# A hybrid recurrent encoder: score matmuls under a high priority, with the backward scores of both halves as one group

## The chip, the cores and the metric

The kernel runs on one core of a Trainium2 chip. The metric is device time in microseconds (us) of one execution. A core has five engines that run their own instruction streams and wait for each other by semaphores: TensorE (PE in the profile, its weight loads PEld), VectorE (DVE), ScalarE (ACT), GpSimd (POOL) and SyncE (SP), which here starts most of the transfers.

## What is computed

Two layers on 1024 tokens of width 1024, in float32. Each projects its input, mixes along the sequence, projects back and adds with a layer norm. The mixers of layer 0 are a dilated window attention (8 heads) and a gated linear attention (GLA, 4 heads with 256 values); the mixer of layer 1 is an HGRN2 recurrence (12 heads with 128 values). GLA and HGRN share this recurrence, run forward and backward:

```python
def _chunk_gated_scan(q, k, v, log_g):
    ...
    b = jnp.cumsum(log_g, axis=2)
    ref = b[:, :, CHUNK // 2 - 1:CHUNK // 2]
    s = jnp.einsum('bnthk,bnshk->bnhts', q * jnp.exp(b - ref), k * jnp.exp(ref - b))
    s = jnp.where(np.tril(np.ones((CHUNK, CHUNK), bool)), s, 0.0)
    o_intra = jnp.einsum('bnhts,bnshv->bnthv', s, v)
    b_last = b[:, :, -1]
    q_dec = q * jnp.exp(b)
    k_dec = k * jnp.exp(b_last[:, :, None] - b)

    def step(state, xs):
        qd, kd, vc, bl = xs
        o = jnp.einsum('bthk,bhkv->bthv', qd, state)
        state = jnp.exp(bl)[..., None] * state + jnp.einsum('bthk,bthv->bhkv', kd, vc)
        return state, o
    ...

def bidirectional_gated_scan(q, k_fwd, g_fwd, k_bwd, g_bwd, v):
    fwd = _chunk_gated_scan(q, k_fwd, v, g_fwd)
    ...
    return fwd + bwd - diag
```

## The kernel before

All weights and activations of the projections are split into a high and a low part, and each product takes three matmuls: L237 to L239 for projections with features on the partitions ("pj"), L249 to L251 for those with tokens there, L271 to L273 for the out-projections ("po"), whose results VectorE adds to the residual (L276). They are most of TensorE's work. ScalarE rounds a raw weight tile (the cast, L199), VectorE makes the low part (L200); ScalarE or VectorE evacuates a finished projection (L712 and others).

The recurrence works on tiles of 128 tokens, in two halves of four tiles (hf 0 and 1) and two directions (d = 1 backward, d = 0 forward). The function `core` of a `ScanHead` gives a list of units in the order (1,1), (1,0), (0,0), (0,1), written (d,hf) from here on. For each come three units, and for d = 0 a fourth:

- `prep`: on VectorE a running sum of the log gate (L743), differences (L746, L750), and scaled queries and keys: qi (L756), ki (L1056 in GLA, L1129 in HGRN), k3 (L787), q1 and k1 (L792, L793), q2 and k2 (L797, L798), q3 (L799). ScalarE makes the exponentials (through L158), GpSimd small factors (L763 to L783). GLA's log gate begins with a matmul (L1044) that takes a bank of the scores' PSUM tag.
- `keys`: three or four transposes of k3 on TensorE (L809, PSUM tag tr, one buffer), a copy of them on ScalarE (L812, k3T), state matmuls (L818, tag kv, one buffer), and the state updates on VectorE (L828 for the first, L830 for the others).
- `scores`: 32 small matmuls (L844) of 32 output partitions each, into one PSUM buffer of the tag s (two buffers). They need ki, qi, k1, q1, k2 and q2, of which k2 is made last. Then S is taken from PSUM: by ScalarE for d = 1 (L870), by VectorE under a mask for d = 0 (L873).
- `output` (d = 0): o from S and v (L888), from the forward states (L890) and the backward ones (L892), tag o; a norm with two matmuls of ones (L905, L906, tag tr) and the multiplication by the gate (L912 to L917).

GLA heads have nbuf = 1 (one buffer for most of these tiles), HGRN heads nbuf = 2. Heads are named H0 to H11 in layer 1 and by their number in GLA; H2, H4, H6, H8 and H10 have an out-projection of the pair of heads before them beside their core, and token projections.

The units of a head's core are merged with the projections of the next heads and the out-projections of earlier ones by a table of fractions (`WIN`, `LAST`, `merge`), which gives the program's order. A scheduler then orders each engine's instructions, once, when the kernel is built: by their place in the program, and earlier than that by up to 3000 places for what stands under `high_priority(offset=3000)`; the evacuations, the weight casts and other short steps are under it before the change, too. On the chip every engine takes its instructions in that order. `issue_after` ties an instruction to come after a named one of the same engine.

Of the kernel before, what the change touches and what calls it, by code (L numbers as in the profile page):

```python
# [2 lines left out]

# [12 lines left out]
P = 128  # L16
# [677 lines left out]
class ScanHead(Item):  # L694
# [135 lines left out]
                    nc.vector.scalar_tensor_tensor(dst, old, r["dec"][:, t, :], kv[:, j, :],  # L830
                                                   op0=ALU.mult, op1=ALU.add)

    def scores(self, d, hf):

        T, nc = self.T, self.T.nc
        mm = nc.tensor.matmul
        r = self.pr[d, hf]
        ev, od = d, 1 - d
        first, last = d, 1 - d
        X = T.ps.tile([P, 4, P], F32, tag="s", name="s", bufs=2)  # L840

        def block(t, s0, t0, n, k, q):

            mm(X[s0:s0 + 32, t, t0:t0 + n], k, q, start=True, stop=True)  # L844

        def far(t, i):

            k2, q2 = (r[x][:, t].rearrange("p a c -> p (a c)") for x in ("k2", "q2"))
            block(t, 64 * first + 32 * i, 64 * last, 64, k2[:, 32 * i:32 * i + 32], q2)

        def near(t, i):

            n = 2 * t + i
            block(t, 64 * i + 32 * ev, 64 * i + 32 * od, 32, r["k1"][:, n, :], r["q1"][:, n, :])

        def own(t, i, e):

            s0 = 64 * i + 32 * e
            t0, n = (s0, 32) if e == ev else (64 * i, 64)
            block(t, s0, t0, n, r["ki"][:, t * P + s0:t * P + s0 + 32], r["qi"][:, t * P + t0:t * P + t0 + n])  # L860

        for t in range(4):
            far(t, ev), far(t, od), own(t, last, ev), own(t, last, od)
            near(t, first), own(t, first, od), near(t, last), own(t, first, ev)
        dst = self.S[:, hf * 4:hf * 4 + 4, :]
        for i in range(2):
            ss = slice(64 * i, 64 * i + 64)
            cs = slice(0, P) if i == first else slice(64 * last, 64 * last + 64)
            if d == 1:
                nc.scalar.copy(dst[ss, :, cs], X[ss, :, cs])  # L870
            else:
                mask = T.mask[ss, cs].unsqueeze(1)
                nc.vector.copy_predicated(out=dst[ss, :, cs], data=X[ss, :, cs],  # L873
                                          mask=mask.broadcast_to([64, 4, cs.stop - cs.start]))

    def output(self, hf):

# [42 lines left out]
    def core(self):  # L920
        pool = self.pool

        def begin():
            if self.mate:
                self.v = self.mate.v
            self.pr = {}
            self.S = pool.tile([P, NT, P], F32, tag="S", name="S", bufs=1)
            self.stb = pool.tile([P, NT - 1, self.V], F32, tag="stb", name="stb", bufs=1)
            self.stf = {}
            self.y, self.held = {}, {}  # L930

        units = [begin, lambda: self.activate(1)]
        for d, hf in ((1, 1), (1, 0), (0, 0), (0, 1)):
            if (d, hf) == (0, 0):
                units.append(lambda: self.activate(0))
            units.append(lambda d=d, hf=hf: self.prep(d, hf))
            units.append(lambda d=d, hf=hf: self.keys(d, hf))
            units.append(lambda d=d, hf=hf: self.scores(d, hf))
            if (d, hf) == (0, 0):
                units.append(lambda: self.activate(2))  # L940
            if d == 0:
                units.append(lambda hf=hf: self.output(hf))
            if (d, hf) == (0, 0):
                n = len(units)
        return units, n / len(units)
# [186 lines left out]
def trunk_kernel(tc, x, x_t, w_in_ab, gla_gate_up, gla_gate_bias, gla_norm, w_out_ab, w_in_c, hgrn_lower_bounds,  # L1132
                 hgrn_norm, w_out_c, rel_bias, ln_gain, ln_bias, onehot, ident, mask, out):
    nc = tc.nc
    with ExitStack() as ctx:
# [127 lines left out]
        def step(items, i, after=None, spill=()):  # L1263
# [6 lines left out]
            late, n = it.late(), it.urgent  # L1270
            m = n + 2 if "LATE2" in w else len(late)
            core, p = it.core()
            st = [(core, 0.0, 1.0), (late[:n], *w["URGENT"]), (late[n:m], *w["LATE"])]
            if late[m:]:
                st.append((late[m:], *w["LATE2"]))
# [93 lines left out]
```

## Time and profile before

| | |
|---|---|
| runs (us) | 1990.79, 1993.53, 1996.21; median 1993.53 |
| profiled execution (us) | 1989.75, its span 1988.0 |
| mean granted clock of TensorE | 0.995 of full |
| busy: TensorE, its weight loads | 1909.4 us (96%), 1568.1 us (79%) |
| busy: VectorE, ScalarE, GpSimd | 1317.6 us (66%), 1015.1 us (51%), 345.8 us (17%) |
| score matmuls (L844) | 64 groups of 32; each matmul shows as two records, 4096 in all |

A time line has a row for each instruction, or for some alike in a row (x3): its start in us from the start of the span, its duration, engine, line, what it writes from what it reads, and in brackets the idle time of its engine just before it with the instruction that ended it. A matmul's duration is modelled and overlaps the next one's, so on TensorE one reads the distance from start to start. The groups by line give busy time, the mean of one and the idle time before them. The chain that ended last is followed back from the last instruction; its shares tell which engine sets the time.

### The profile page before, as it was taken

How to read it: one execution, taken by the hardware profiler on the slowest of the kernel's cores; microseconds unless marked ns; L12 is line 12 of the kernel's file. 1: busy time of each engine (PE TensorE's matmuls, PEld its weight loads, DVE VectorE, ACT ScalarE, POOL GpSimd, SP SyncE). 2: the span in 40 equal slices, each digit the busy share in tenths (PEclk: the TensorE clock that was granted, in tenths of full speed). 3: DMA queues.
4: the chain of work that ended last, by engine and by line, in shares of the span. 5: the costliest groups of instructions: out<-in, count | busy, mean ns of one | idle time of the engine just before them, and what ended most of it. 6: DMA issues, size and time to landing. Idle time of an engine off the chain costs nothing.

```text
span 1988.0 us, 35443 instructions
## 1 busy us (share of the span) xinstructions
PE 1909.4 (96%) x13887; PEld 1568.1 (79%) x13887; DVE 1317.6 (66%) x2757; ACT 1015.1 (51%) x1851; POOL 345.8 (17%) x856
## 2 busy tenths in 40 slices
PE   7999999999999999989899999999999999999997
PEld 4777777787787878867778888888888888888875
DVE  4687878775776575677667646655764664666477
ACT  5665666653554343444556445535544642654473
POOL 0210202001211011121423111111311210131133
PEclk9999999999999999999999999999999999999999
DMA  8321212123121212112311211121121112012112
GB/s 230 76 50 38 45 38 44 33 75 100 38 54 49 70 49 70 48 43 75 123 39 43 69 54 38 39 80 33 33 85 44 33 49 75 27 39 90 38 44 85
DMA packets 142868, 118.60 MB, mean 60 GB/s; under 512 B 15302, under 2 KB 122566, under 8 KB 142700
## 3 DMA queue, kind: packets, MB, share of 16 engines
q1 hardware_dynamic: 128875, 98.36, 16.9%
q0 software_dynamic: 4512, 11.47, 2.3%
q10 hardware_dynamic: 9312, 6.50, 1.1%
q8 instruction: 109, 1.79, 0.4%
q14 instruction: 60, 0.48, 0.1%
HBM read 108.19 MB, written 8.11 MB: 59 GB/s over the span
## 4 chain that ended last, share of the span: by engine, by line
PE 46%; DVE 8%; ACT 4%; DMA 2%; issue 2%; POOL 1%; DVEq 0%; ACTq 0%; POOLq 0%
PE pj L237 9%; PE pj L238 8%; PE pj L239 8%; PE kv L818 3%; DVE g L743 2%; PE po L271 2%; PE po L272 2%; PE po L273 2%; PE s L844 2%; PE pj L249 1%; PE pj L250 1%; PE pj L251 1%; PE o L888 1%; PE o L892 1%; PE o L890 1%
## 5 line engine op out<-in xcount | busy, mean ns | idle before, releaser
L237 PE MATMUL pj<-xH,wH 128*128 128x512 f32 x1280 | 510.7, 399 | 5.0 <-DVE kl L531 2.3
L238 PE MATMUL pj<-xL,wH 128*128 128x512 f32 x1280 | 506.3, 396 | 0.0
L239 PE MATMUL pj<-xH,wL 128*128 128x512 f32 x1280 | 505.7, 395 | 0.0
L199 ACT CAST wH<-wraw 128x512 fp32r<-128x512 f32 x248 | 153.6, 619 | 298.8 <-PE pj L238 180.0
L200 DVE TENSOR_TENSOR wL<-wraw,wH 128x512 fp32r<-128x512 f32 x248 | 172.4, 695 | 200.6 <-ACT wH L199 187.9
L237 PEld LDWEIGHTS pj<-xH,wH 128*128 128x128 f32 x1280 | 240.6, 188 | 53.2 <-issue 3.0
L239 PEld LDWEIGHTS pj<-xH,wL 128*128 128x128 f32 x1280 | 240.7, 188 | 45.5
L238 PEld LDWEIGHTS pj<-xL,wH 128*128 128x128 f32 x1280 | 240.9, 188 | 44.3 <-DVE xL L348 0.4
L763 POOL TENSOR_TENSOR eT<-gE 128x16 f32<-128x16 f32 x64 | 29.6, 463 | 1037.0 <-ACT gE L158 1037.0
L249 PE MATMUL pj<-wH,xH 128*128 128x256 f32 x640 | 182.1, 285 | 2.3 <-ACT E L712 1.9
L250 PE MATMUL pj<-wL,xH 128*128 128x256 f32 x640 | 180.8, 283 | 0.0
L251 PE MATMUL pj<-wH,xL 128*128 128x256 f32 x640 | 180.6, 283 | 0.0
L276 DVE TENSOR_TENSOR z<-z,po 128x512 f32<-128x512 f32 x200 | 134.9, 682 | 65.1 <-PE po L273 64.2
L271 PE MATMUL po<-woH,yH 128*128 128x512 f32 x336 | 138.4, 421 | 9.4 <-ACT woH L217 5.8
L272 PE MATMUL po<-woL,yH 128*128 128x512 f32 x336 | 134.7, 401 | 0.5 <-DVE woL L218 0.5
L273 PE MATMUL po<-woH,yL 128*128 128x512 f32 x336 | 132.1, 394 | 0.0
L249 PEld LDWEIGHTS pj<-wH,xH 128*128 128x128 f32 x640 | 122.1, 191 | 6.2 <-ACT E L712 2.3
L250 PEld LDWEIGHTS pj<-wL,xH 128*128 128x128 f32 x640 | 122.1, 191 | 2.9
L251 PEld LDWEIGHTS pj<-wH,xL 128*128 128x128 f32 x640 | 122.0, 191 | 2.6
L271 PEld LDWEIGHTS po<-woH,yH 128*128 128x128 f32 x336 | 61.8, 188 | 33.4 <-ACT woH L217 10.7
L818 PE MATMUL kv<-v,k3T 128*128 128x128 f32 (+1 forms) x448 | 80.0, 313 | 8.1 <-DVE stb L830 5.2
L217 ACT CAST woH<-wraw 128x512 fp32r<-128x512 f32 x80 | 47.5, 617 | 78.2 <-PE po L273 26.7
(230 smaller groups left out, 3852.7 us busy)
## 6 DMA issues: line engine op xcount, KB each, us to landing
wraw<-in_w_in_c_dram SPq DMA_DIRECT2D x152, 256.0 KB, 2.9
wraw<-in_w_in_ab_dram SPq DMA_DIRECT2D x96, 256.0 KB, 2.9
wraw<-in_w_out_c_dram SPq DMA_DIRECT2D x44, 256.0 KB, 2.7
wraw<-in_w_out_ab_dram SPq DMA_DIRECT2D x40, 256.0 KB, 2.6
z<-in_x_dram ACTq DMA_DIRECT2D x8, 512.0 KB, 5.6
strip<-line POOLq DMA_DIRECT2D x8, 448.0 KB, 5.7
park<-sp SPq DMA_DIRECT2D x14, 256.0 KB, 2.0
out_dram<-z SPq DMA_DIRECT2D x6, 512.0 KB, 2.6
```

The source lines that it names most:

```text
L199: self.nc.scalar.copy(h, raw)
L200: self.nc.vector.tensor_tensor(lo, raw, h.bitcast(F32), op=ALU.subtract)
L237: mm(ps[:m], wH, xH[:, k, :], start=(k == 0), stop=False)
L238: mm(ps[:m], wH, xL[:, k, :], start=False, stop=False)
L239: self.lastmm = mm(ps[:m], wL, xH[:, k, :], start=False, stop=(k == last)).ins
L249: self.nc.tensor.matmul(o, xH, wH, start=(k == 0 and i % 2 == 0), stop=False)
L250: self.nc.tensor.matmul(o, xH, wL, start=False, stop=False)
L251: self.lastmm = self.nc.tensor.matmul(o, xL, wH, start=False, stop=(k == KT - 1 and i % 2 == 1)).ins
L271: mm(ps, yH[:, ts], h, start=(b == 0), stop=False)
L272: mm(ps, yH[:, ts], lo, start=False, stop=False)
L273: mm(ps, yL[:, ts], h, start=False, stop=(b == nb - 1))
L818: nc.tensor.matmul(kv[:, j, :], k3T[:, t, :], self.val(hf * 4 + t), start=True, stop=True)
```

## The change

The matmuls of `scores` come under the high priority, tied in order by `issue_after`, so that no other matmul comes between those of a group; the copies from PSUM to S are made after it, at the program's own place. For nbuf = 2 (HGRN) and d = 1, one unit after `prep` and `keys` of (1,0) issues the scores of (1,0) and then those of (1,1).

```diff
--- before.py
+++ after.py
@@ -1,5 +1,5 @@
 import math
-from contextlib import ExitStack
+from contextlib import ExitStack, nullcontext
 
 import concourse.bass as bass
 import concourse.tile as tile
@@ -830,10 +830,19 @@
                     nc.vector.scalar_tensor_tensor(dst, old, r["dec"][:, t, :], kv[:, j, :],
                                                    op0=ALU.mult, op1=ALU.add)
 
-    def scores(self, d, hf):
+    def scores(self, d, hfs):
+
+        tc, done = self.T.tc, []
+        with tc.high_priority(offset=3000):
+            for hf in hfs:
+                with tc.issue_after(self.lastmm) if done else nullcontext():
+                    done.append(self.score_tiles(d, hf))
+        for fn in done:
+            fn()
+
+    def score_tiles(self, d, hf):
 
         T, nc = self.T, self.T.nc
-        mm = nc.tensor.matmul
         r = self.pr[d, hf]
         ev, od = d, 1 - d
         first, last = d, 1 - d
@@ -841,7 +850,7 @@
 
         def block(t, s0, t0, n, k, q):
 
-            mm(X[s0:s0 + 32, t, t0:t0 + n], k, q, start=True, stop=True)
+            self.lastmm = nc.tensor.matmul(X[s0:s0 + 32, t, t0:t0 + n], k, q, start=True, stop=True).ins
 
         def far(t, i):
 
@@ -862,16 +871,20 @@
         for t in range(4):
             far(t, ev), far(t, od), own(t, last, ev), own(t, last, od)
             near(t, first), own(t, first, od), near(t, last), own(t, first, ev)
-        dst = self.S[:, hf * 4:hf * 4 + 4, :]
-        for i in range(2):
-            ss = slice(64 * i, 64 * i + 64)
-            cs = slice(0, P) if i == first else slice(64 * last, 64 * last + 64)
-            if d == 1:
-                nc.scalar.copy(dst[ss, :, cs], X[ss, :, cs])
-            else:
-                mask = T.mask[ss, cs].unsqueeze(1)
-                nc.vector.copy_predicated(out=dst[ss, :, cs], data=X[ss, :, cs],
-                                          mask=mask.broadcast_to([64, 4, cs.stop - cs.start]))
+
+        def take():
+            dst = self.S[:, hf * 4:hf * 4 + 4, :]
+            for i in range(2):
+                ss = slice(64 * i, 64 * i + 64)
+                cs = slice(0, P) if i == first else slice(64 * last, 64 * last + 64)
+                if d == 1:
+                    nc.scalar.copy(dst[ss, :, cs], X[ss, :, cs])
+                else:
+                    mask = T.mask[ss, cs].unsqueeze(1)
+                    nc.vector.copy_predicated(out=dst[ss, :, cs], data=X[ss, :, cs],
+                                              mask=mask.broadcast_to([64, 4, cs.stop - cs.start]))
+
+        return take
 
     def output(self, hf):
 
@@ -935,7 +948,9 @@
                 units.append(lambda: self.activate(0))
             units.append(lambda d=d, hf=hf: self.prep(d, hf))
             units.append(lambda d=d, hf=hf: self.keys(d, hf))
-            units.append(lambda d=d, hf=hf: self.scores(d, hf))
+            both = self.nbuf == 2 and d == 1
+            if not both or hf == 0:
+                units.append(lambda d=d, hfs=(0, 1) if both else (hf,): self.scores(d, hfs))
             if (d, hf) == (0, 0):
                 units.append(lambda: self.activate(2))
             if d == 0:
```

The scheduler turns this into the following moves. TensorE in head H3, just ahead of the backward scores (pj are projections for later heads, tr the transposes of k3). Before, the group of (1,1) follows its transposes:

```order
L238 MATMUL pj<-xL,wH 128x512
L239 MATMUL pj<-xH,wL 128x512
L809 MATMUL tr<-ident,k_12895 128x128 x4
L844 MATMUL s<-q_12901,k_12902 32x64 x2
L844 MATMUL s<-qi,ki 32x32
L844 MATMUL s<-qi,ki 32x64
L844 MATMUL s<-q_12897,k_12898 32x32
```

With the change the joined group comes first (its first matmul reads k2 of (1,0)):

```order
L237 MATMUL pj<-xH,wH 128x512
L238 MATMUL pj<-xL,wH 128x512
L853 MATMUL s<-q_12988,k_12989 32x64 x2
L853 MATMUL s<-qi,ki 32x32
L853 MATMUL s<-qi,ki 32x64
L853 MATMUL s<-q_12984,k_12985 32x32
```

and the transposes of (1,1) come behind it, among projections:

```order
L238 MATMUL pj<-xL,wH 128x512
L239 MATMUL pj<-xH,wL 128x512
L809 MATMUL tr<-ident,k_12895 128x128 x4
L237 MATMUL pj<-xH,wH 128x512
L238 MATMUL pj<-xL,wH 128x512
```

The joined group moved ahead of the transposes; counted in projections from the (0,1) group of the head before, it stands at the 111th and the transposes at the 127th, where they and the first scores stood at the 120th. The norm's matmuls of the head before (L905, L906 of its second half) end at the 22nd instead of the 16th.

VectorE in H3, from the first state update of (1,1) on (stb are the backward states, g the log gates that the next preparation sums). Before:

```order
L828 COPY stb<-kv 128x128
L830 SCALAR_TENSOR_TENSOR stb<-stb,dec,kv 128x128
L743 SCALAR_TENSOR_TENSOR g<-restart,g 128x512
L830 SCALAR_TENSOR_TENSOR stb<-stb,dec,kv 128x128
L746 COPY gt<-g 128x32
L743 SCALAR_TENSOR_TENSOR g<-restart,g 128x512
L830 SCALAR_TENSOR_TENSOR stb<-stb,dec,kv 128x128
L750 TENSOR_TENSOR g<-g,gt 128x16x16
L746 COPY gt<-g 128x32
L750 TENSOR_TENSOR g<-g,gt 128x16x16
```

With the change:

```order
L828 COPY stb<-kv 128x128
L743 SCALAR_TENSOR_TENSOR g<-restart,g 128x512
L830 SCALAR_TENSOR_TENSOR stb<-stb,dec,kv 128x128
L746 COPY gt<-g 128x32
L743 SCALAR_TENSOR_TENSOR g<-restart,g 128x512
L830 SCALAR_TENSOR_TENSOR stb<-stb,dec,kv 128x128
L750 TENSOR_TENSOR g<-g,gt 128x16x16
L830 SCALAR_TENSOR_TENSOR stb<-stb,dec,kv 128x128
L746 COPY gt<-g 128x32
L750 TENSOR_TENSOR g<-g,gt 128x16x16
```

The first scan (L743) now stands ahead of the second update, and an L750 ahead of the fourth.

TensorE in H3, in the middle of the (0,1) group. Before, three state matmuls cut it:

```order
L844 MATMUL s<-qi,ki 32x64
L844 MATMUL s<-q_13315,k_13316 32x32
L844 MATMUL s<-qi,ki 32x32
L818 MATMUL kv<-v,k3T 128x128 x3
L844 MATMUL s<-q_13319,k_13320 32x64 x2
L844 MATMUL s<-qi,ki 32x32
L844 MATMUL s<-qi,ki 32x64
L844 MATMUL s<-q_13315,k_13316 32x32
```

With the change its end and what follows are:

```order
L853 MATMUL s<-q_13315,k_13316 32x32
L853 MATMUL s<-qi,ki 32x64
L853 MATMUL s<-q_13315,k_13316 32x32
L853 MATMUL s<-qi,ki 32x32
L905 MATMUL o<-q_12981,stb 128x128
L901 MATMUL o<-S,v 128x128
L903 MATMUL o<-q_13156,stf 128x128
L905 MATMUL o<-q_12981,stb 128x128
```

Over the whole program the 64 groups stand in 78 pieces before and in 52 with the change, none of them cut by another matmul. Here the group is in one piece, stands between output matmuls of (0,0), and the three state matmuls come later.

## Rows read from the trace of the kernel before

**Rows 1.** The page, busy time by engine, and the chain that ended last by engine:

```profile
PE 1909.4 (96%) x13887; PEld 1568.1 (79%) x13887; DVE 1317.6 (66%) x2757; ACT 1015.1 (51%) x1851; POOL 345.8 (17%) x856
...
PE 46%; DVE 8%; ACT 4%; DMA 2%; issue 2%; POOL 1%; DVEq 0%; ACTq 0%; POOLq 0%
```

**Rows 2.** Groups by line, shapes apart: busy us, mean ns | idle before, and its releasers:

```profile
L844 PEld LDWEIGHTS s<-q,k 128*32 128x32 f32 x2048 | 62.1, 110 | 19.7 <-issue 16.1 <-DVE k L798 0.8 <-PE pj L238 0.7
...
L818 PE MATMUL kv<-v,k3T 128*128 128x128 f32 x336 | 49.4, 287 | 8.1 <-DVE stb L830 5.2 <-ACT k3T L812 0.8 <-ACT S L870 0.4
...
L809 PE MATMUL tr<-ident,k 128*128 128x128 f32 x224 | 35.5, 275 | 11.5 <-DVE k L787 11.5
```

**Rows 3.** Time line of TensorE, scores of (1,0), H2: start us, us, work:

```profile
1193.30 0.40 PE L239 MATMUL pj<-xH,wL 128*128 128x512 f32 x1
1193.62 0.25 PE L844 MATMUL s<-q,k 128*32 128x64 f32 x2
...
1194.54 0.23 PE L844 MATMUL s<-qi,ki 128*32 128x32 f32 x2
1194.69 0.50 PE L237 MATMUL pj<-xH,wH 128*128 128x512 f32 x1
1195.03 0.39 PE L238 MATMUL pj<-xL,wH 128*128 128x512 f32 x1
1195.26 0.40 PE L239 MATMUL pj<-xH,wL 128*128 128x512 f32 x1
```

**Rows 4.** The same, the split (0,1) group of H2:

```profile
1204.35 0.24 PE L844 MATMUL s<-qi,ki 128*32 128x64 f32 x3
1204.73 0.94 PE L818 MATMUL kv<-v,k3T 128*128 128x128 f32 x6
```

**Rows 5.** Time line of all engines, preparation and (1,1) of H3:

```profile
1214.96 0.62 ACT L199 CAST wH<-wraw 128x512 fp32r<-128x512 f32 x1 [0.26 <-PE pj L238]
...
1215.49 0.59 ACT L712 ACTIVATE E<-pj 128x512 f32<-128x512 f32 x1
...
1234.72 0.39 PE L237 MATMUL pj<-xH,wH 128*128 128x512 f32 x1
...
1234.78 0.42 DVE L798 TENSOR_TENSOR k<-ki,Gk 128x256 f32<-128x256 f32 x1
...
1236.77 0.60 PE L809 MATMUL tr<-ident,k 128*128 128x128 f32 x4
```

**Rows 6.** The same, H4, a head with an out-projection:

```profile
1313.20 0.28 PE L249 MATMUL pj<-wH,xH 128*128 128x256 f32 x1
...
1313.55 0.42 DVE L798 TENSOR_TENSOR k<-ki,Gk 128x256 f32<-128x256 f32 x1
```

**Rows 7.** The same, H0:

```profile
1001.64 0.42 DVE L798 TENSOR_TENSOR k<-ki,Gk 128x256 f32<-128x256 f32 x1
...
1003.16 0.60 PE L809 MATMUL tr<-ident,k 128*128 128x128 f32 x4
```

**Rows 8.** The same, state matmuls and updates of (1,1) and (1,0), H3:

```profile
1243.36 1.16 PE L818 MATMUL kv<-v,k3T 128*128 128x128 f32 x8
...
1245.14 1.22 DVE L743 TENSOR_TENSOR_SCAN g<-restart,g 128x512 f32<-128x512 uint8 x1
...
1247.75 0.32 DVE L830 SCALAR_TENSOR_TENSOR stb<-stb,dec,kv 128x128 f32<-128x128 f32 x1
...
1247.99 0.42 DVE L750 TENSOR_TENSOR g<-g,gt 128x256 f32<-128x256 f32 x1
...
1248.22 0.91 PE L818 MATMUL kv<-v,k3T 128*128 128x128 f32 x6 [0.49 <-DVE stb L830]
```

**Rows 9.** TensorE's waits in GLA, and a window (us, busy by engine, granted clock):

```profile
706.39 0.52 PE L809 MATMUL tr<-ident,k 128*128 128x128 f32 x3 [1.02 <-DVE k L787]
...
902.73 0.80 PE L888 MATMUL o<-S,v 128*128 128x128 f32 x2 [2.65 <-DVE S L873]
...
904.00:912.00 8.00, 7.24 (x48) 6.96 (x47) 7.40 (x7) 4.13 (x8) 6.75 (x4) 0.74 0.12 36
```

## The prediction

> **What bounds the kernel now.** I read the page first, then the groups by line, then time lines of single heads. TensorE is busy 96% of the span, and it holds 46% of the chain that ended last, VectorE 8% [rows 1]: the kernel is a stream of TensorE instructions in one fixed order, and time changes only where that stream waits or changes from one kind of matmul to another. So I look for such places. The weight loads of the score matmuls waited for k2 (L798) 0.8 us in the whole run; the 16.1 us beside it are "issue", a price of changing kind and no wait for data [rows 2]. The transposes waited 11.5 us for k3 (L787), the state matmuls 8.1 us, mostly for the state updates on VectorE (L830) that free their one PSUM buffer [rows 2].
>
> **The change, part by part.** The order shows that it adds and removes no instruction on any engine. Score groups move on TensorE, and copies and parts of preparation move on VectorE and ScalarE behind them. I cost places, not instructions.
>
> *Changes of kind.* Projection to projection takes 0.23 us from start to start; projection to score 0.32, the last score to a projection 0.15 where one score after another takes 0.03 (all 32 start between 1193.62 and 1194.54), and the step behind that 0.34 [rows 3]. One excursion so costs 0.10 on the way in and twice 0.11 on the way out, 0.32 in all. Joining the two backward groups of an HGRN head saves one excursion. But the order shows what comes back: the transposes of (1,1), which led straight into its scores, now stand between projections (+0.12), one state matmul of (0,0) is left alone behind its scores (+0.18), and (0,1) goes into the outputs at other points (+0.07). I take 0 for the head; the ends are -0.3 and +0.2, or -3.6 to +2.4 over 12 heads.
>
> The Trainium skill's page "TensorEngine Tiling (Array Packing)", Key Properties, says that changing the tiling mode drains TensorE. By that every one of the 26 pieces fewer (78 to 52) would pay, 8.3 us at 0.32 from this trace; the neighbours that lose contact are then left out. That is rival 2.
>
> *The split groups.* In 11 HGRN heads the (0,1) group was cut in two by three state matmuls: from the last score start to the first state matmul 0.38 us, against 0.15 where a projection follows [rows 3, 4]. The 0.2 us more is a wait for the copy of the transposes. It goes: 11 x -0.2 = -2.2. Three split GLA groups at 0.3 each: -0.9.
>
> *The wait of the joined group.* This is the largest term. In the order it stands nine projections ahead of the place where the (1,1) transposes stood, and it needs k2 of both halves. In head H3 the transposes started at 1236.77; the ninth projection before them started at 1234.72, where the group now stands, plus 0.10 for the change of kind 1234.83. The k2 of (1,0) ends at 1234.78 + 0.42 = 1235.20, and a matmul starts about 0.1 after its releaser: a wait of 0.47 [rows 5]. But this chain of preparation begins with ScalarE's evacuation of E at 1215.49 and ends 19.7 us later, and what stands before that evacuation on ScalarE is the norm of the head before (L905, L906, then L158), whose matmuls stand six projections later: 6 x 0.23 = 1.36, of which ScalarE's idle 0.26 takes up some [rows 5]; I take +1.05. So 1.5 us in each of H1, H3, H5, H7, H9, whose distances agree. In the heads with an out-projection the group comes after the 53rd of 92 token projections: at 1313.20 in H4, with k2 at 1313.97, so 0.7 for H2, H4, H6, H10 and nothing for H8 [rows 6]. H0: 14 projections before 1003.16 is 1000.0, k2 is ready at 1002.06, so 2.1 [rows 7]. H11: 0.5. Sum 7.5 + 2.8 + 2.1 + 0.5 = +12.9. Lower end: preparation moves up with its reader, because ScalarE and VectorE have free time, 0; upper end: 2.1 in each of 11 heads, +23. I take the middle, because H3's own rows give it. What is queued behind the waiting group is all of TensorE, so each wait is time lost in full, and the weight casts and evacuations that wait for projections shift with it.
>
> *The state matmuls of (1,0).* They need the PSUM buffer that the fourth update of (1,1) frees. Now four of them start at 1243.36 and the next three at 1248.22, after a wait of 0.49; the third L830 begins at 1247.75 [rows 8]. In the new order a scan (L743, 1.22 us) stands before the first L830 instead of behind it, and an L750 of 0.42 before the last. On TensorE the three now arrive 4.15 us after the four (four matmuls, three transposes, 12 projections), and the updates finish about 5.1 after. The wait grows by about 0.4, the L750 alone: 11 x 0.4 = +4.4; ends 0 (VectorE catches up) and +1.2 each (a whole scan, +13).
>
> *GLA.* A head's preparation starts from a gate matmul (L1044) that shares the score tag, and the transposes then wait for k3: 1.02 us at 706.39, 11.5 in all [rows 2, 9]. With scores earlier the gate matmul of the next half is issued earlier or later by a few projections. Counted in the order at 0.23 each: H0 -1.4, H1 -0.8, H2 -0.2, H3 -1.4 net (a wait of 1.6 goes, 1.3 comes with three residual additions that land in the chain): -3.8; ends -8 and +2.
>
> *End of GLA.* The last forward group is followed by a wait of 2.65 us for the masked copy (L873), and the granted clock is 0.74 of full between 904 and 912, so for a part of it the lower of its two levels, after that idle time [rows 9]. The last scores stand about 4 us earlier, but VectorE is busy 7.40 of the 8 us there [rows 9], so their copies can't go far ahead. I take -0.5; ends -6 (wait and slow stretch both go) and +2.
>
> Sum: 12.9 + 4.4 - 2.2 - 0.9 - 3.8 - 0.5 + 0 = **+9.9 us**. The profiled execution took 1989.75, which is 3.8 below the median of the three runs, 1993.53. On the median: **2003.4**.
>
> **The rivals.** 1. *The joined group does not wait.* Preparation has slack in every head and finishes in time. For: before, scores almost never waited for k2 [rows 2], and the 0.47 that H3's rows give directly is small. Against: that they stood nine projections later. Then 9.9 - 12.9 = -3.0, or 1990.5, which is no change. The bound where it decides: k2 has to be ready 1.5 us sooner in H1 to H9.
>
> 2. *Changes of kind decide, with the GLA end.* 26 pieces fewer at 0.32 are -8.3, and the 2.65 us wait with its slow stretch (-6) goes. With the waits of the joined group at a third (+4.3), and the terms of the updates, the transposes' copy and the gates as in the sum (+4.4 - 2.2 - 3.8), that is 4.3 + 4.4 - 2.2 - 3.8 - 8.3 - 6 = -11.6, or 1982. For: each excursion does cost 0.3 [rows 3]. Against: the order puts transposes and single state matmuls where pieces vanished. It decides if TensorE's waits before the joined group sum to less than 5 us.
>
> 3. *The forward groups wait too.* By my walk through the new order the scores of (0,0) and (0,1) come just as their k2 is ready, within 0.3 us. If the preparation runs late by 0.5 there in 20 groups, +10 more: 2013.
>
> 4. *Nothing moves.* The priority only regroups what TensorE does anyway: 1993.5.
>
> **How the numbers follow.** My forecast has 0.48, rival 1 0.25, rival 2 0.15, rival 3 0.07, rival 4 0.05. About 0.3% (6 us) is what a measurement of this kernel can tell from no change. Of the forecast, 0.42 lies over +6 us and 0.06 below, since the waits can be half of what I take; rival 1 gives 0.22 to no change and 0.03 to faster. Slower: 0.42 + 0.07 = 0.49. Same: 0.06 + 0.22 + 0.05 = 0.33. Faster: 0.03 + 0.15 = 0.18. The forecast's own range is 1996 to 2012 (joined group 6 to 20 us). To hold 8 in 10 the range takes in rival 1 and most of rival 3 and leaves rival 2 out: 1988 to 2013.
>
> **What would show it.** In the profile of the changed kernel the weight loads of the score line should wait for L798 about 13 us, in some 11 instances of 0.5 to 2 us, and the state matmuls should wait for the updates some 9 instead of 5 us; TensorE's transposes should wait less than 11.5 us for L787 (8 or less). Busy time of TensorE should stay within a few us of before. The prediction is wrong if score loads wait under 5 us for k2 and the time is at or below 1990, or if new waits show at the outputs (L888) or the norm (L905).

## The result, and the profile after

The changed kernel takes 2017.45 us (median of 6 runs, 2009.15 to 2020.53), the kernel before 1993.59 (6 runs, 1990.79 to 1996.21). The ratio is 1.0121, 95% interval [1.0109, 1.0132]: slower by 23.9 us. I forecast slower by 9.9 and a range that ended at 2013. The direction is right, the size is not. The profiled execution took 2017.65 us, its span is 2015.5, its mean granted clock 0.990.

On the page, busy time by engine and the chain that ended last by engine:

```profile
PE 1913.0 (95%) x13887; PEld 1574.5 (78%) x13887; DVE 1314.8 (65%) x2757; ACT 1014.0 (50%) x1851; POOL 335.5 (17%) x856
...
PE 8%; DVE 2%; ACT 1%; DMA 1%; issue 0%; POOL 0%; DVEq 0%; ACTq 0%
```

TensorE's busy time is 3.6 us longer than before [rows 1], the span 27.5: the loss is waiting, not work. The chain is broken off early here (its shares sum to some 12%), so it tells nothing; the groups by line tell more (busy us, mean ns | idle before, and what ended it):

```profile
L853 PE MATMUL s<-q,k 128*32 128x64 f32 x1024 | 66.6, 228 | 15.0 <-DVE k L798 14.7 <-ACT z L391 0.2
...
L853 PEld LDWEIGHTS s<-q,k 128*32 128x32 f32 x2048 | 64.2, 113 | 26.9 <-DVE k L798 19.7 <-issue 2.0 <-PE tr L809 1.9
...
L818 PE MATMUL kv<-v,k3T 128*128 128x128 f32 x336 | 53.5, 293 | 11.5 <-DVE gt L746 8.3 <-ACT k3T L812 1.4 <-DVE stb L830 0.8
...
L809 PE MATMUL tr<-ident,k 128*128 128x128 f32 x224 | 36.0, 277 | 11.8 <-DVE k L787 11.6 <-DVE xL L348 0.2
```

The score matmuls, which hardly waited for k2 [rows 2], now wait 14.7 us for it (L798), in 14 instances: 13.6 us in the twelve joined groups of HGRN, and 0.55 in each of two GLA halves. Their weight loads wait 19.7. The state matmuls wait 11.5 instead of 8.1 us. The transposes wait 11.6 instead of 11.5 us; a gain in GLA that I had counted on does not show in the sum.

Time lines of ScalarE, TensorE and VectorE of the changed kernel, where the joined group of H3 starts:

```profile
1227.19 0.62 ACT L199 CAST wH<-wraw 128x512 fp32r<-128x512 f32 x1 [0.48 <-PE pj L238]
1227.72 0.59 ACT L712 ACTIVATE E<-pj 128x512 f32<-128x512 f32 x1
...
1245.13 0.39 PE L238 MATMUL pj<-xL,wH 128*128 128x512 f32 x1
...
1246.99 0.42 DVE L798 TENSOR_TENSOR k<-ki,Gk 128x256 f32<-128x256 f32 x1
...
1247.46 0.25 PE L853 MATMUL s<-q,k 128*32 128x64 f32 x2 [1.95 <-DVE k L798]
```

This is [rows 5] again: from the evacuation of E at 1227.72 to the end of L798 at 1247.41 it is 19.7 us, as before. The projection at 1245.13 is the last ahead of the group, so scores could have started near 1245.46 (0.23 for the projection, 0.10 for the change of kind), and they started at 1247.46: 2.0 us lost, where I took 1.5. ScalarE's idle time before the weight cast did not take up part of the later norm, as I had assumed; it grew from 0.26 to 0.48, since the cast waits for a projection. Counted from the start of the kernel the place is plainer: before, k2 of (1,0) in H3 was finished when 3450 projections had started, and the joined group now stands behind the 3440th. I had counted from the (0,1) group of the head before, which itself moved up by seven. The five heads H1, H3, H5, H7 and H9 all show the same 1.95. H0 and H4 [rows 6, 7]:

```profile
1009.62 0.41 DVE L798 TENSOR_TENSOR k<-ki,Gk 128x256 f32<-128x256 f32 x1
...
1010.09 0.25 PE L853 MATMUL s<-q,k 128*32 128x64 f32 x2 [1.04 <-DVE k L798]
...
1327.57 0.42 DVE L798 TENSOR_TENSOR k<-ki,Gk 128x256 f32<-128x256 f32 x1
...
1328.04 0.25 PE L853 MATMUL s<-q,k 128*32 128x64 f32 x2 [0.43 <-DVE k L798]
```

1.04 in H0 (I took 2.1), 0.43 in H4 (I took 0.7). No score group of the forward halves of HGRN waits for k2, so rival 3 falls. State matmuls and updates in H3:

```profile
1261.17 0.29 DVE L828 COPY stb<-kv 128x128 f32<-128x128 f32 x1 [2.36 <-PE kv L818]
1261.38 1.22 DVE L743 TENSOR_TENSOR_SCAN g<-restart,g 128x512 f32<-128x512 uint8 x1
...
1264.22 0.42 DVE L750 TENSOR_TENSOR g<-g,gt 128x256 f32<-128x256 f32 x1
1264.56 0.34 DVE L830 SCALAR_TENSOR_TENSOR stb<-stb,dec,kv 128x128 f32<-128x128 f32 x1
...
1265.05 0.91 PE L818 MATMUL kv<-v,k3T 128*128 128x128 f32 x6 [0.83 <-DVE gt L746]
```

This is [rows 8] with the scan ahead of the second update and L750 ahead of the fourth: the state matmuls wait 0.83 instead of 0.49. (The row names L746 as the one that ended the wait; it stands right behind the fourth L830, which frees the buffer, and ends no earlier.)

The end of GLA, a row of TensorE and a window (busy us of TensorE, its loads, VectorE, ScalarE, GpSimd; then granted clock):

```profile
910.87 1.11 PE L343 MATMUL tr<-ident,z 128*128 128x128 f32 x4 [6.43 <-POOL z L393]
...
904.00:912.00 8.00, 1.55 (x8) 0.95 (x7) 5.17 (x11) 4.47 (x10) 2.90 (x2) 0.73 0.24 76
```

The wait of 2.65 us at the outputs [rows 9] is gone, and the next reader waits instead: the transposes of the normalized rows (L343) wait 6.43 for the layer norm on GpSimd (L393), and the low clock in this window stays, 0.73 against 0.74. In the net this costs nothing: the last projection ahead of the end of GLA comes 4.7 us later than in the trace of before, the first one behind it 4.6.

### The profile page after: what moved, and what is told of

It is laid out like the page before. It is cut to its first block, busy times and chain, and to the rows that moved or that the text cites. A ratio compares the mean times of both kernels' runs of the same rounds, so it can differ in the third digit from the quotient of the medians.

```text
span 2015.5 us, 35424 instructions
## 1 busy us (share of the span) xinstructions
PE 1913.0 (95%) x13887; PEld 1574.5 (78%) x13887; DVE 1314.8 (65%) x2757; ACT 1014.0 (50%) x1851; POOL 335.5 (17%) x856
## 5 line engine op out<-in xcount | busy, mean ns | idle before, releaser
L763 POOL TENSOR_TENSOR eT<-gE 128x16 f32<-128x16 f32 x64 | 34.9, 546 | 1063.5 <-ACT gE L158 1063.5
L818 PE MATMUL kv<-v,k3T 128*128 128x128 f32 (+1 forms) x448 | 85.5, 320 | 11.8 <-DVE gt L746 8.3
L218 DVE TENSOR_TENSOR woL<-wraw,woH 128x512 fp32r<-128x512 f32 x80 | 54.6, 703 | 61.8 <-ACT woH L217 61.2
```

## The experiments

The kernel before ran beside the first four at 1992.38 us and beside the others at 1992.12 (medians of 25 runs each); the ratios are to these.

| kernel | median us | ratio to before | 95% interval |
|---|---|---|---|
| late11: joined group behind the transposes of (1,1) | 1996.44 | 1.0021 | [1.0011, 1.0031] |
| split: priority, halves apart | 2015.59 | 1.0114 | [1.0098, 1.0131] |
| noprio: joined, no priority | 1995.20 | 1.0013 | [1.0004, 1.0022] |
| gla_only: priority in GLA alone | 1996.35 | 1.0019 | [1.0010, 1.0029] |
| late10h: HGRN only, joined group behind the transposes of (1,0) | 1990.89 | 0.9995 | [0.9985, 1.0006] |
| tied10: no priority, joined and tied | 1989.44 | 0.9996 | [0.9986, 1.0005] |
| scan1: tied10, and one running sum later | 1987.55 | 0.9982 | [0.9970, 0.9994] |
| again: the changed kernel, one run | 2015.92 | | |

**late11.** The only edit: the joined group may not be issued ahead of the transposes of (1,1).

```diff
-                with tc.issue_after(self.lastmm) if done else nullcontext():
+                with tc.issue_after(self.lastmm) if done else (tc.issue_after(self.lasttr[1, 1]) if len(hfs) == 2 else nullcontext()):
...
-            nc.tensor.transpose(tp[:, t, :], r["k3"][:, t * P:(t + 1) * P], T.ident)
+            self.lasttr[d, hf] = nc.tensor.transpose(tp[:, t, :], r["k3"][:, t * P:(t + 1) * P], T.ident).ins
```

> Theory A: most of the loss is the wait of the joined backward group for the k2 of (1,0) (about 15 us in the changed kernel), with the longer wait of the state matmuls behind it (3.8 us) and stretches at the lower clock that follow some of those waits (about 1.5 us each). Here the joined group is tied behind the transposes of (1,1), everything else stays: score matmuls wait under 3 us for L798; the three state matmuls of (1,0) come 9 instead of 12 projections behind the four, so their wait may grow by up to 0.7 in 11 heads; time 1998 to 2008. Theory B, that the forward groups, the norm and the copies which the priority moved cost the time: 2012 to 2018.

Measured 1996.44, 21.0 us below the changed kernel (19.8 when each is taken from the kernel before that ran beside it) and 1.6 below the range that I expected. Its groups by line:

```profile
L853 PEld LDWEIGHTS s<-q,k 128*32 128x32 f32 x2048 | 61.6, 110 | 11.7 <-issue 4.0 <-DVE k L798 1.9 <-PE tr L809 1.9
...
L818 PE MATMUL kv<-v,k3T 128*128 128x128 f32 x336 | 52.7, 291 | 8.4 <-DVE gt L746 6.9 <-DVE stb L830 0.7 <-ACT g L158 0.6
...
L809 PE MATMUL tr<-ident,k 128*128 128x128 f32 x224 | 36.3, 279 | 12.9 <-DVE k L787 12.3 <-DVE xL L348 0.2
```

The score matmuls no longer wait for k2 (1.9 us on the weight loads), the rest of the change is in it, and only 4 us of its loss are left, about as much as the priority costs in GLA alone (gla_only, below). So theory A holds and B falls: the place of the joined group is what cost most. The state matmuls still wait 8.4 us, but not the 11.5 of the changed kernel, and a small wait of the (0,0) transposes comes up behind them, as in head H5:

```profile
1426.02 0.91 PE L818 MATMUL kv<-v,k3T 128*128 128x128 f32 x6 [0.70 <-DVE gt L746]
...
1431.26 0.63 PE L809 MATMUL tr<-ident,k 128*128 128x128 f32 x4 [0.44 <-DVE k L787]
```

**split.**

```diff
-            both = self.nbuf == 2 and d == 1
+            both = False
```

> The priority as in the change, each half a group of its own in HGRN too. Theory A (the priority puts scores at a place where k2 is not made yet): both halves still wait, (1,1) about 1.0 and (1,0) about 0.3 to 1 us in H1 to H9, 12 more excursions at 0.32; time 2013 to 2021. Rival C, that the joining of the halves is to blame: score waits under 4 us, 1995 to 2003.

Measured 2015.59, as theory A has it. In H3 the scheduler puts (1,1) 16 projections and (1,0) five or so ahead of where the joined group stood, and each waits for its own k2:

```profile
1245.04 0.25 PE L853 MATMUL s<-q,k 128*32 128x64 f32 x2 [1.46 <-DVE k L798]
...
1249.14 0.25 PE L853 MATMUL s<-q,k 128*32 128x64 f32 x2 [0.25 <-DVE k L798]
```

1.46 and 0.25, with one more change of kind about what the joined group loses in one piece. So joining is not to blame (rival C falls here); the place is, to which the priority takes scores while k2 is not made.

**noprio.**

```diff
-        with tc.high_priority(offset=3000):
+        with nullcontext():
```

> Halves joined as in the change, no priority. Theory A: the joined group stands right behind the transposes of (1,1), waits for k2 under 2 us; only one scan stands before the fourth update, so the state matmuls' wait falls from 5 to under 2 us: 1988 to 1995. Rival C (joining is to blame by itself, as both score buffers are taken at once and the copies come late): 2003 or more.

Measured 1995.20, 0.2 above the range of A and far from rival C. The joined group lands right behind the transposes of (1,1) here too, by the program's own order. My second expectation failed: the order of VectorE did change, but the state matmuls wait 7.1 us for the updates by the waits of its trace, not under 2, as only nine projections and three transposes now lie between the two groups of them, where before a score group lay there, too.

**gla_only.**

```diff
-        with tc.high_priority(offset=3000):
+        with tc.high_priority(offset=3000) if self.nbuf == 1 else nullcontext():
...
-            both = self.nbuf == 2 and d == 1
+            both = False
```

> The priority in the four GLA heads alone; HGRN is issued as before the change. From the two traces I read about +2 us in GLA up to the norm and -0.7 at its end: 1993 to 1998. My forecast had -5.2 for this part: 1988. Rival D, that the end of GLA with its new wait for the normalized rows (6.6 us, L393 to L343) is a large part of the loss: 2000 or more.

Measured 1996.35, or +3.8 us (2.0 to 5.8 by the interval), where my forecast had -5.2 for this part. TensorE's rows: two of a (0,1) half, whose scores now stand right behind their transposes, the one at the end of GLA, one in the layer norm behind it, and then the transposes' group by line:

```profile
765.99 0.55 PE L809 MATMUL tr<-ident,k 128*128 128x128 f32 x3 [0.60 <-DVE k L787]
767.09 0.25 PE L853 MATMUL s<-q,k 128*32 128x64 f32 x2 [0.55 <-DVE k L798]
...
909.85 1.12 PE L343 MATMUL tr<-ident,z 128*128 128x128 f32 x4 [6.20 <-POOL z L393]
...
964.96 1.09 PE L343 MATMUL tr<-ident,z 128*128 128x128 f32 x4 [2.26 <-DVE xL L348]
...
L809 PE MATMUL tr<-ident,k 128*128 128x128 f32 x224 | 35.6, 275 | 9.7 <-DVE k L787 9.5 <-DVE xL L348 0.2
```

The transposes' waits fell by 2.0 us (11.5 to 9.5), half of what I counted. In two halves (near 647 and 767) the scores then wait 0.55 for k2, which is made after k3, behind a wait of the transposes that was not there before. At the end L343 waits 6.20. Rival D is not borne out by the time (2000 or more). Where the loss arises can be read by comparing the start of the same projection in this trace and in that of before. This trace is 1.6 us late ahead of GLA, 3.9 at the last projection ahead of its end, and 3.6 at the first behind it: the wait of 6.20 took the place of others, and my -0.5 for the end was about right. The next 3.0 us come by 961 us, where the transposes wait 2.26 for the residual (L348). In the trace of before this wait was 1.09:

```profile
960.68 0.63 PE L343 MATMUL tr<-ident,z 128*128 128x128 f32 x4 [1.09 <-DVE xL L348]
```

A stretch of 3.4 us at the lower clock, which before has not, begins there too, at 964.65 (granted clock 0.58 from 964 to 968). The trace of late11 has the wait (2.26) and no such stretch, and loses 1.7 at this place. So the 3.8 lies partly in GLA and partly in the layer norm behind it; this was read from single traces and not tried apart.

**late10h.** GLA as before the change, the priority in HGRN, and the joined group tied behind the transposes of (1,0).

```diff
-        with tc.high_priority(offset=3000):
+        with tc.high_priority(offset=3000) if self.nbuf == 2 else nullcontext():
...
-                with tc.issue_after(self.lastmm) if done else nullcontext():
+                with tc.issue_after(self.lastmm) if done else (tc.issue_after(self.lasttr[1, 0]) if len(hfs) == 2 else nullcontext()):
```

> Priority in HGRN only, GLA as before the change, the joined group tied behind the transposes of (1,0), so between them and their state matmuls. Theory A: score matmuls wait under 2 us for L798; the joined group fills the time in which the state matmuls wait for the updates, as the (1,0) group did before, so that wait is about 0.6 in 11 heads or less; GLA's +4 us of the priority are gone; time 1987 to 1994. Theory B (the priority's moves of forward groups and norms cost the time): 1998 or more.

Measured 1990.89, the same as before. With the joined group where its inputs are ready and GLA untouched, the priority itself costs nothing that shows in HGRN; theory B falls a second time. It gains nothing either.

**tied10.** No priority; the joined group is tied as in late10h, and the (0,1) group of HGRN may not be issued ahead of its own state matmuls, so nothing cuts it.

```diff
-        with tc.high_priority(offset=3000):
+        with nullcontext():
...
-                with tc.issue_after(self.lastmm) if done else nullcontext():
+                with tc.issue_after(self.lastmm) if done else (tc.issue_after(self.lasttr[1, 0]) if len(hfs) == 2 else (tc.issue_after(self.lastkv) if self.nbuf == 2 and hfs == (1,) else nullcontext())):
...
-                nc.tensor.matmul(kv[:, j, :], k3T[:, t, :], self.val(hf * 4 + t), start=True, stop=True)
+                self.lastkv = nc.tensor.matmul(kv[:, j, :], k3T[:, t, :], self.val(hf * 4 + t), start=True, stop=True).ins
```

> No priority; the joined group behind the transposes of (1,0), the (0,1) group of HGRN tied behind its own state matmuls, so that nothing cuts it. 55 pieces as in the kernel before it. If changes of kind cost 0.32 each in the net, this is about 23 pieces x 0.32 = 7 us and 11 x 0.2 of transposes' copies below before: 1982 to 1987. If the neighbours give it back, as I took it in the forecast: 1988 to 1993.

Measured 1989.44, ratio 0.9996 with no change in its interval: 23 pieces fewer (55 against 78) are not worth 7 us; the interval reaches from 2.8 us below before to 1.0 above, and the state matmuls wait only 1.1 us more than before (9.2 against 8.1). That bears out the forecast's zero for the changes of kind and speaks against rival 2. That the next place pays what one saves is a reading: the "issue" idle of the score loads falls from 16.1 to 6.4 us, and that of the state matmuls' loads rises from under 0.8 to 11.5.

**scan1.** tied10, and the running sum of (0,1) is tied behind the last state update of (1,1).

```diff
-        nc.vector.tensor_tensor_scan(run, T.restart, run, 0.0, op0=M, op1=ALU.add)
+        with T.tc.issue_after(self.lasttr['u11']) if self.nbuf == 2 and d == 0 and hf in (1,) else nullcontext(): nc.vector.tensor_tensor_scan(run, T.restart, run, 0.0, op0=M, op1=ALU.add)
...
-                    nc.vector.scalar_tensor_tensor(dst, old, r["dec"][:, t, :], kv[:, j, :],
+                    self.lasttr['u%d%d' % (d, hf)] = nc.vector.scalar_tensor_tensor(dst, old, r["dec"][:, t, :], kv[:, j, :],
...
```

> As tied10, and the running sum of (0,1) (L743, 1.22 us) is tied behind the last state update of (1,1), so that the PSUM buffer of the state matmuls comes free earlier. If the state matmuls of (1,0) wait for what VectorE does ahead of the fourth update: their wait falls from 5 to 8 us to under 1.5, and the time is 4 to 7 us below tied10. If their wait is for something else: as tied10 within 2 us.

Measured 1987.55, the one kernel whose interval lies below 1 (0.9982 [0.9970, 0.9994]). Groups by line of tied10:

```profile
L818 PE MATMUL kv<-v,k3T 128*128 128x128 f32 x336 | 49.5, 287 | 9.2 <-DVE gt L746 6.4 <-ACT k3T L812 1.0 <-ACT qi L158 0.9
...
L809 PE MATMUL tr<-ident,k 128*128 128x128 f32 x224 | 35.9, 277 | 11.0 <-DVE k L787 11.0
```

and of scan1:

```profile
L818 PE MATMUL kv<-v,k3T 128*128 128x128 f32 x336 | 49.5, 287 | 2.6 <-ACT k3T L812 1.0 <-ACT qi L158 0.9
...
L809 PE MATMUL tr<-ident,k 128*128 128x128 f32 x224 | 36.2, 278 | 14.2 <-DVE k L787 14.2
```

The state matmuls' wait for what VectorE does ahead of the fourth update is gone (6.4 us to nothing; 2.6 in all are left), which shows its cause. But the transposes now wait 14.2 instead of 11.0: the preparation of the forward halves became late next. Of 6.6 us taken away 3.2 came back there, and the medians differ by 1.9, under the 4 to 7 I expected and hardly clear of the spread of the ten runs each.

**again.** The changed kernel a second time.

> The changed kernel a second time. The waits of the joined group are in the program: the same instances within 0.1 us, 14 to 16 us in all. Theory A2 (part of the loss is the lower clock, at places that change from run to run): the stretches at half clock within HGRN lie elsewhere or are more or fewer, and the time follows them, about 1.7 us for each stretch of 3.4. Rival: the stretches are at the same places, right behind the same two waits.

One run of 2015.92. The score matmuls wait 14.2 us for k2. The five waits of 1.95 are the same to 0.01 us, but those of H4, H6, H8 and H10 differ by up to 0.3, more than the 0.1 that I expected. The run was for the low clock. Windows of the changed kernel (us, busy time of TensorE, its loads, VectorE, ScalarE, GpSimd; then granted clock, DMA), around the joined groups of H5 and H7, and behind that of H9:

```profile
1415.00:1419.00 4.00, 2.82 (x13) 2.00 (x11) 3.74 (x9) 0.60 (x1) 3.13 (x8) 1.00 0.17 51
1419.00:1423.00 4.00, 3.23 (x133) 3.02 (x134) 1.31 (x4) 2.00 (x5) 0.00 (x0) 1.00 0.01 4
1589.00:1593.00 4.00, 2.05 (x49) 1.47 (x49) 3.72 (x8) 0.31 (x1) 1.80 (x5) 1.00 0.00 0
1593.00:1597.00 4.00, 4.00 (x106) 3.55 (x99) 0.00 (x0) 2.20 (x5) 0.00 (x0) 0.59 0.02 4
...
1768.00:1772.00 4.00, 4.00 (x131) 3.85 (x123) 0.28 (x1) 1.53 (x4) 0.00 (x0) 0.60 0.02 4
```

TensorE stood for 1.95 us ahead of each group. Behind the wait of H5 the clock stays at 1.00; behind those of H7 and H9 it is 0.59 and 0.60, the lower of the two levels for 3.4 us. What that costs is the distance from the group to the state matmuls of (1,0), the same instructions in both heads (TensorE's rows, H5 and then H7):

```profile
1419.77 0.25 PE L853 MATMUL s<-q,k 128*32 128x64 f32 x2 [1.95 <-DVE k L798]
...
1437.35 0.91 PE L818 MATMUL kv<-v,k3T 128*128 128x128 f32 x6 [0.83 <-DVE gt L746]
...
1592.43 0.25 PE L853 MATMUL s<-q,k 128*32 128x64 f32 x2 [1.95 <-DVE k L798]
...
1611.52 0.91 PE L818 MATMUL kv<-v,k3T 128*128 128x128 f32 x6 [0.81 <-DVE gt L746]
```

17.58 us in H5, 19.09 in H7: 1.5 for one such stretch. In the second run of the same kernel it followed the wait of H5, too:

```profile
1415.00:1419.00 4.00, 2.05 (x65) 1.51 (x65) 3.46 (x8) 0.04 (x1) 1.53 (x5) 1.00 0.00 0
1419.00:1423.00 4.00, 4.00 (x89) 3.58 (x80) 0.00 (x0) 2.22 (x5) 0.00 (x0) 0.57 0.02 4
...
1593.00:1597.00 4.00, 4.00 (x66) 3.46 (x58) 0.32 (x1) 2.48 (x5) 0.00 (x0) 0.57 0.01 4
...
1768.00:1772.00 4.00, 4.00 (x100) 3.67 (x93) 0.00 (x0) 2.36 (x5) 0.00 (x0) 0.68 0.02 4
```

and the same distance there is 19.08:

```profile
1418.16 0.25 PE L853 MATMUL s<-q,k 128*32 128x64 f32 x2 [1.95 <-DVE k L798]
...
1437.24 0.91 PE L818 MATMUL kv<-v,k3T 128*128 128x128 f32 x6 [0.82 <-DVE gt L746]
```

So the stretches recur at places behind the joined group's wait, H7 and H9 in both runs and H5 in one; the rival of this expectation is the better one, and A2's "other places" holds for H5 alone. In the profiles of the kernels without that wait (before, late11, noprio, gla_only, late10h, tied10, scan1) no stretch at the lower clock lies between 1000 and 1940 us, nor in split, whose longest wait for k2 there is 1.47. (At the end of HGRN late10h and tied10 have one each, at 1943.80 and 1945.91, and the two runs of the changed kernel have one, too, at 1969.16 and 1965.15.) The waits come first and the low clock behind them; that the wait causes it is the plain reading, not something I could turn on and off by itself.

## Why the prediction was wrong in size

*What bounds the kernel*: right. Busy time stayed, waits moved.

*The wait of the joined group*: right in mechanism and nearly in size, 12.9 forecast, 13.6 measured in HGRN. The total is nearer than its parts, which is luck: 2.0 instead of 1.5 in the odd heads H1 to H9, half of what I took in H0, and of the even heads H8, for which I took nothing, waits 0.49. The step that was mis-sized is ScalarE's idle time, which I let take up some of the later norm. late11 takes the wait away by place alone. Rivals 1 and 4 fall by the same rows.

*The state matmuls of (1,0)*: +4.4 forecast; the idle time of this group rose from 8.1 to 11.5, so +3.4. Right. The -2.2 for the split groups stands beside it: a wait of 0.14 us for the copy of the transposes is gone in 11 heads, 1.5 us in all, and this is part of the same idle time. No run shows the rest of the 2.2.

*Changes of kind*: taken as 0. tied10 bears that out to 2.8 us (0.14%); rival 2 fell. The sentence of the Trainium skill (page "TensorEngine Tiling (Array Packing)", Key Properties) that a change of mode drains TensorE agrees with the single excursion of [rows 3], but counting pieces by it would have given -8.3 where no run shows a gain. My reading of the 16.1 us of "issue" [rows 2] as a price is not borne out either: it fell to 2.0 with the change and to 6.4 in tied10, which is not shown to be faster.

*GLA*: this is the first step that failed, -3.8 for the chain, -0.9 for the split groups and -0.5 for the end, where gla_only measures +3.8. I counted how far the gate matmul moves in the order and booked each projection as time gained by the transposes. The gain was half of it, and I did not ask what waits next: scores right behind transposes need k2, which is made after k3, and the transposes in the layer norm behind GLA wait 2.26 instead of 1.09. The end itself was about right (-0.3 in the trace). What else loses time inside GLA stays open. I gave the chain no end as far out as this: my upper end was +2.

*What was missing*: the lower clock behind the joined group's waits, two stretches of 1.5 us in one run, three in the other, so 3.0 to 4.5 us. I looked at the clock only at the end of GLA, where the trace of before had a low stretch with a 2.65 us wait [rows 9]; I did not carry that reading over to the eleven waits that I myself added.

With the measured sizes the sum closes, as far as terms read from single traces can. The joined groups in HGRN 13.6, the state matmuls with the copies 3.4, GLA 3.8 (the 1.1 us that its scores wait for k2 are in it) and the clock 3.0 to 4.5 are 23.8 to 25.3, against 23.9. Of the 14.0 us that the forecast missed, 9.0 so lie in GLA, 3.0 to 4.5 in the clock, 1.2 in the state matmuls and copies together (3.4 against 4.4 - 2.2), and 0.7 in the joined group. The step to late11 checks it without GLA: 13.4 less wait for k2 in HGRN, 3.1 less at the state matmuls and the 3.0 to 4.5 of the clock are 19.5 to 21.0, where 19.8 to 21.0 were measured.

## What to carry to other kernels

A priority in a static order can move an instruction up to a place where its inputs are not made yet. On an engine that is busy 96% of the time the wait was lost in full here, once per head. Check for each hoisted group which input is made last, by its end in the trace, and tie the group behind an instruction that is as late as that, as late11 and late10h did. Count its place from something that the change does not move. When you add waits, price the low clock that may follow them from a place in the trace where one did, and when you take one away, find the reader that waits next.

## What I had not expected of the hardware

After 1.95 us of standing TensorE's granted clock fell to the lower level for 3.4 us behind some of five waits of the same length (H7 and H9 in both runs, H5 in one, H1 and H3 in none), at 1.5 us each. The start of the kernel also differs from run to run, in a part that no edit touches: the profile of before has no stretch at the lower clock in the first 60 us, the changed kernel has one of 3.4 us at 50.9 and split one of 6.8 at 24.1 and one of 3.4 at 54.8. At the 160th of TensorE's projection steps, long ahead of the first score, the changed kernel is 2.3 us later than before and split 7.1. A difference of some us between two single profiles says little without a look at these places.
